# Hybrid decoder trunk, two layers: router by token blocks, the second adaLN's sums moved into mixing, a float32 gather and a 19th weight slot

## The chip, the cores and the metric

One core of one Trainium2 chip runs the whole program. Times are device microseconds (us) of one execution; the median of three executions is given beside the one that was profiled.

Engines: TensorE (PE, with its weight loads shown apart as PEld), VectorE (DVE), ScalarE (ACT), GpSimd (POOL) and SyncE (SP). SP's queue issues all transfers of weights; DMA engines move the bytes.

## What is computed

Two layers over 256 tokens of width 1024, all in float32:

```python
for l in range(DEPTH):
    mod = (silu(c) @ w_ada[l] + b_ada[l])[:, None, :]
    sh1, sc1, gt1, sh2, sc2, gt2 = jnp.split(mod, 6, axis=-1)
    h = x * (1 + sc1) + sh1
    q, k, v, u, vs = jnp.split(h @ w_in[l], split_at, axis=-1)
    att = rms_norm(diff_attention(rope(q), rope(k), v, lam), subln_g[l]) * (1.0 - lam_init)
    sg = chunk_spatial_gate(gelu(u), gelu(vs), sg_ln_g[l], sg_ln_b[l], w_spatial[l], b_spatial[l])
    mix = jnp.concatenate([att, sg], axis=-1) @ w_out[l]
    x = layer_norm(DEEPNORM_ALPHA * x + (1 + gt1) * mix, ln1_g[l], ln1_b[l])
    h = x * (1 + sc2) + sh2
    ffn = hier_moe(h, ...)      # top 1 of 4 groups, then top 2 of its 8 experts, SwiGLU with 512 inner columns
    x = layer_norm(DEEPNORM_ALPHA * x + (1 + gt2) * ffn, ln2_g[l], ln2_b[l])
```

The weights of all 32 experts of a layer are 6 MiB each, so nearly all of the 468 MB that are moved are expert weights.

## The kernel before

**Weights.** All weights form one list of transfers of up to 1 MiB (`stream`), in the order in which the program uses them. `pump` (the `dma_start` of line 180) puts them into a ring of `RING = 18` slots, in the order of the list: transfer n waits for the release of a slot, which `done` reports when the last reader of an older transfer has been issued. An expert without tokens is skipped on the chip by a condition on its transfers. The list of a layer is: w_in by sections (Q, K, VS, U, V), pieces of w_ada between them, w_out, more of w_ada, and then the experts' gate, up and down weights.

**Tokens.** The 256 tokens are two blocks of 128 (`tci` 0 and 1), a token a partition. `X` holds them as [128, 2, 8, 128]: column d = 8p + k of a token stands at [k, p], so that a fixed k gives 128 contiguous numbers, and the view `Xn` that goes over a token's 512 columns in natural order has a stride. `transpose_X` turns X into blocks with 128 columns on partitions, and `make_hT` applies adaLN's scale and shift in the copy out of PSUM, shared between DVE and ACT.

**Mixing.** `mixing` runs the sections (L594), attention and gating, and then the output projection `wo` (L861): 16 records per pair (`tci`, `hf`), first those that read gating (`hf` = 1) for both blocks, with `att_T` (L737, L738) between, then those that read attention. `residual` (L887, L889) multiplies by the gate and adds to X, `normalise` takes the statistics (L556) and normalises in place (L558).

**adaLN.** c times a w_ada column piece is a sum over 1024 rows. One part is folded ahead of time on DVE (`ada_fold`, L446: a scaled addition of one 512-column piece to an accumulator, done a few at a time by `fold_on`) or on POOL (`ada_fold_too`), the other is summed on PE (`ada_sum`: L411 for the accumulator, L416 for the rest). `ada_cols` turns the row into columns by transposes (L430), `affine_cols` makes scale and shift (`gc`, `bc`) of them. For the second adaLN (`s2`) four of eight pieces are folded in `mixing`, and `routing` does the rest.

**Routing and gather.** `routing` makes, between the normalised X and the router's logits: s2's sums and columns; a split of X into three bfloat16 parts (`Xp`; casts on ACT L920 to L937, subtractions on POOL L922 to L938), which together are X to float32's accuracy; the transposed hT; the logits with the router's 36 columns stationary and 256 tokens moving (L944), over two halves of the partitions, which are copied (L946, L947) and added by a matmul with the constant `fold` (L952); and the copy of the logits (L955). Then DVE finds the chosen experts and each token's position in its expert's slots. `selection` makes 0/1 matrices `G` (L1124), and `gather` multiplies the three parts of X by G (L1150) and applies gc and bc on the way out of PSUM (L1156 on DVE, L1159 on ACT).

**Experts.** `experts` runs 11 units: six of 2 experts with 64 slots each, then five of 4 experts with 32. A unit does gate and up (`proj`, L1171), silu and product (L1215, L1225), transposes (L1237, L1239), down (L1259), the multiplication by the gate (L1265) and the scatter back to the tokens (L1180). `gather` for the next two units follows the gate of every odd unit. `rescale` and `add_x` (L1187, alpha X through PE into the same sum) come in the last units. `spill` is the branch for experts with more tokens than slots; it isn't taken with these inputs.

Of the kernel before, what the change touches and what calls it, by code (L numbers as in the profile page):

```python
# [8 lines left out]
F32 = mybir.dt.float32  # L9
# [3 lines left out]
ALU = mybir.AluOpType  # L13
# [5 lines left out]
RING = 18  # L19
# [8 lines left out]
def kernel(  # L28
# [105 lines left out]
    for l in range(L):  # L134
# [26 lines left out]

    def pump(limit=RING):
# [48 lines left out]
    X = const.tile([P, NTC, KD, P], F32, name="X")  # L211
    fp = front_pool(0)
    xin = fp.tile([P, NTC, D], F32, tag="hT", name="xin")
    def Xn(tci, half=None):
        v = X[:, tci] if half is None else X[:, tci, :, half * 64:(half + 1) * 64]
        return v.rearrange("t k p -> t p k")
# [5 lines left out]
    for tci in range(NTC):  # L222
        nc.sync.dma_start(xin[:, tci, :], x[0, tci * P:(tci + 1) * P, :])
# [48 lines left out]
    fold = const.tile([P, NG + NE], F32, name="fold")  # L272
    V.tensor_tensor(fold, ident[:, 0:NG + NE], ident[:, 64:64 + NG + NE], op=ALU.add)
# [163 lines left out]
    def ada_fold(l, part):  # L437
        acc = held["ada", l, part, 0][:, 0, :]
        for k in range(4):
# [112 lines left out]
    def normalise(tci):  # L552
        st = small.tile([P, 2, 6], F32, tag="bnst", name="bnst")
        flat = X[:, tci].rearrange("t k p -> t (k p)")
        for h in range(2):
            V.bn_stats(st[:, h, :], flat[:, h * 512:(h + 1) * 512])  # L556
        mu, rs = mean_rstd(st)
        V.tensor_scalar(flat, flat, mu, rs, op0=ALU.subtract, op1=ALU.mult)  # L558


    def normalise_psum(tci, ps, st):
# [3 lines left out]
        S.activation(Xn(tci, 1), ps[1].rearrange("t (p k) -> t p k", k=KD), AF.Identity, scale=rs, bias=nm)  # L565
        V.tensor_scalar(Xn(tci, 0), ps[0].rearrange("t (p k) -> t p k", k=KD), mu, rs,  # L566
# [21 lines left out]
    def mixing(l, fp, y_prev, sts):  # L588
        hT = fp.tile([P, KD, NT], F32, tag="hT", name="hT")
# [797 lines left out]
```

## Time and profile before

| | |
|---|---|
| median of three executions | 1234.27 us (1232.76 to 1234.47) |
| the profiled execution | 1234.19 us |
| its span in the trace | 1232.57 us |
| PE busy | 1052.1 us (85%) |
| DVE busy | 347.1 us (28%) |
| ACT busy | 169.5 us (14%) |
| POOL busy | 73.2 us (6%) |
| DMA | 467.62 MB, mean 379 GB/s |

The span is what the trace covers; 1.6 us of the execution lie around it. The busy shares are means over stages that have different limits, so the views that count are those by stretch (busy time of each engine, granted PE clock, share of the DMA engines and GB/s) and the timeline, in which a row is a run of like instructions with its start, its length, its count and, in brackets, the idle time of the engine ahead of it and what released it.

Layer 0 lies about from 0 to 620 us, layer 1 from there to the end. In each the mixing comes first (to about 175 and 755 us), then routing (to about 198 and 778 us), then the experts.

### The profile page before, as it was taken

What the parts mean: (1) busy time and instruction counts of PE and PEld (TensorE: products, weight loads), DVE (VectorE), ACT (ScalarE), POOL (GpSimd) and SP (SyncE); (2) the same over time, 40 slices, a digit from 0 to 9 for tenths busy, and PEclk for the clock granted to TensorE, in tenths of its full rate; (3) what the DMA queues carried; (4) which work ended last, traced back from release to release, by engine and by line L of the source; (5) the groups of instructions that cost most, each with busy time, mean ns of one, the idle gap of its engine ahead of it and who ended that gap; (6) DMA issues with size and microseconds to landing.
All of it is one profiled execution on the core that took longest, in us unless ns stands there. A gap on an engine that the chain in (4) does not pass through costs nothing. (4 is left out here: it accounts for less than half of the span.)

```text
span 1232.6 us, 14266 instructions
## 1 busy us (share of the span) xinstructions
PE 1052.1 (85%) x5318; PEld 417.9 (34%) x5320; DVE 347.1 (28%) x803; ACT 169.5 (14%) x401; POOL 73.2 (6%) x52
## 2 busy tenths in 40 slices
PE   5999798899999686778789997989999868778875
PEld 1465343434343131122234653443434213112221
DVE  0386357412111010031045546631112101003103
ACT  1135513101010010000021322210101001000000
POOL 0204511000000000000000302000000000000000
PEclk8899898999999898999999999999999989898998
DMA  9998778899999999999999927889999999999995
GB/s 354 365 409 307 294 280 349 347 405 420 422 420 422 421 421 421 421 422 420 400 396 397 388 86 276 348 343 403 422 421 421 420 422 420 421 421 421 420 411 201
DMA packets 89262, 467.62 MB, mean 379 GB/s; under 512 B 12301, under 2 KB 12817, under 8 KB 40290
## 3 DMA queue, kind: packets, MB, share of 16 engines
q1 hardware_dynamic: 88818, 465.85, 93.6%
q8 instruction: 45, 0.74, 0.2%
q10 hardware_dynamic: 288, 0.52, 0.1%
q0 software_dynamic: 80, 0.26, 0.1%
q14 instruction: 31, 0.25, 0.1%
HBM read 484.43 MB, written 1.05 MB: 394 GB/s over the span
## 5 line engine op out<-in xcount | busy, mean ns | idle before, releaser
L1259 PE MATMUL dps<-w,eaT_moe 128*32 128x512 f32 (+1 forms) x1024 | 202.2, 648 | 45.7 <-DMA w<-in_w_down_dram 36.9
L1171 PE MATMUL up<-w,XT_moe 128*32 128x512 f32 (+1 forms) x1024 | 188.9, 620 | 33.0 <-DMA w<-in_w_up_dram 33.0
L1171 PE MATMUL gate<-w,XT_moe 128*32 128x512 f32 (+1 forms) x1024 | 187.5, 644 | 26.6 <-DMA w<-in_w_gate_dram 26.6
L594 PE MATMUL sec<-w,hT_front 128*128 128x512 f32 x256 | 115.8, 606 | 3.8 <-DVE X L566 2.2
L1259 PEld LDWEIGHTS dps<-w,eaT_moe 128*32 128x32 f32 (+1 forms) x1024 | 53.2, 127 | 177.1 <-issue 98.9
L1171 PEld LDWEIGHTS up<-w,XT_moe 128*32 128x32 f32 (+1 forms) x1024 | 51.4, 123 | 160.5 <-issue 99.3
L1171 PEld LDWEIGHTS gate<-w,XT_moe 128*32 128x32 f32 (+1 forms) x1024 | 52.7, 127 | 155.0 <-issue 105.7
L1225 DVE TENSOR_TENSOR act_moe<-sg_moe,up 128x512 f32<-128x512 f32 x22 | 15.1, 688 | 315.2 <-PE up L1171 280.5
L1265 DVE TENSOR_TENSOR eo_moe<-dps,gt 128x512 f32<-128x512 f32 x44 | 30.4, 692 | 213.6 <-PE dps L1259 213.6
L1180 PE MATMUL y<-eo_moe,wt_moe 128*128 128x512 f32 x176 | 84.9, 607 | 1.6 <-DVE eo_moe L1265 1.6
L1215 ACT ACTIVATE sg_moe<-gate 128x512 f32<-128x512 f32 x22 | 13.1, 597 | 412.6 <-PE gate L1171 412.5
L594 PEld LDWEIGHTS sec<-w,hT_front 128*128 128x128 f32 x256 | 48.6, 195 | 61.8 <-issue 53.9
L1150 PE MATMUL gps<-G_moe,Xp_moe 128*128 128x256 bf16 (+1 forms) x672 | 64.6, 250 | 3.7 <-DVE XT_moe L1156 1.8
L1156 DVE TENSOR_SCALAR XT_moe<-gps,gc,bc 128x128 f32<-128x128 f32 x88 | 30.6, 404 | 120.8 <-PE gps L1150 120.8
L1150 PEld LDWEIGHTS <-Xp_moe 128*128 128x128 bf16 x672 | 53.1, 97 | 22.0 <-issue 13.1
L1195 ACT COPY wt_moe<-wtps 128x256 f32<-128x256 f32 x22 | 8.2, 372 | 275.1 <-PE wtps L1193 275.1
L1180 PEld LDWEIGHTS y<-eo_moe,wt_moe 128*128 128x128 f32 x176 | 30.3, 191 | 43.6 <-issue 40.2
L1159 ACT ACTIVATE XT_moe<-gps,bc,gc 128x128 f32<-128x128 f32 x88 | 33.7, 455 | 41.9 <-PE gps L1150 41.9
L462 POOL TENSOR_TENSOR w<-w,w 128x2048 f32<-128x2048 f32 x7 | 31.6, 4521 | 56.2 <-ACT w L458 45.6
L416 PE MATMUL ada_s<-w,csl 128*32 128x512 f32 x128 | 20.8, 765 | 12.8 <-DMA w<-in_w_ada_dram 12.8
L861 PE MATMUL wo<-w,zu_front 128*128 128x512 f32 x64 | 30.6, 635 | 0.0
L755 PE MATMUL u<-hT_front,w 128*128 128x256 f32 x128 | 28.8, 379 | 0.0
(275 smaller groups left out, 762.2 us busy)
## 6 DMA issues: line engine op xcount, KB each, us to landing
w<-in_w_gate_dram SPq DMA_DIRECT2D x128, 1024.0 KB
w<-in_w_up_dram SPq DMA_DIRECT2D x128, 1024.0 KB
w<-in_w_down_dram SPq DMA_DIRECT2D x120, 1024.0 KB
w<-in_w_ada_dram SPq DMA_DIRECT2D x48, 1024.0 KB
w<-in_w_in_dram SPq DMA_DIRECT2D x20, 1024.0 KB
w<-in_w_out_dram SPq DMA_DIRECT2D x8, 1024.0 KB
w<-in_w_down_dram SPq DMA_DIRECT2D x16, 512.0 KB
xin_front<-in_x_dram SPq DMA_DIRECT2D x2, 512.0 KB
```

Source lines behind the costliest of these rows:

```text
L416: T.matmul(ps[32 * j:32 * j + 32], cs(k), held["ada", l, part, k][:, 0, j * 512:(j + 1) * 512], start=(k == 0), stop=(k == KD - 1))
L462: G.tensor_tensor(acc, acc, w, op=ALU.add)
L594: T.matmul(ps, hT[:, k, tci * P:(tci + 1) * P], held["in", l, s, k // 4][:, k % 4, :], start=(k == 0), stop=(k == KD - 1))
L755: T.matmul(ps[:, 0:NT], held["in", l, U_, k // 4][:, k % 4, g * P:(g + 1) * P], hT[:, k, :], start=(k == 0), stop=(k == KD - 1))
L861: T.matmul(o_ps[tci][h], (cat, zu)[hf][:, kk, tci * P:(tci + 1) * P], w[:, kk, :], start=(hf == 1 and kk == 0), stop=(hf == 0 and kk == 3))
L1150: T.matmul(ps[:, k - kk].rearrange("p j s -> p (j s)"), parts[:, a, tci, k, :], g[:, tci, js[0] * P:(js[-1] + 1) * P], start=(a == 0 and t ...
L1156: V.tensor_scalar(dst, ps[:, k - kk, i, :], gc[:, k:k + 1], bc[:, k:k + 1], op0=ALU.mult, op1=ALU.add)
L1159: S.activation(dst, ps[:, k - kk, i, :], AF.Identity, scale=gc[:, k:k + 1], bias=bc[:, k:k + 1])
L1171: T.matmul(ps[c0:c0 + w], xt[:, k, c0:c0 + w], held[nm, l, place, k // 4][:, k % 4, :], start=(k == 0), stop=(k == KD - 1))
L1180: T.matmul(y[tci][h], wt[:, tci, :], eo[:, h, :], start=(i == 0), stop=(i == NU - 1))
L1259: T.matmul(dps[h][s0:s0 + w], aT[:, kk, s0:s0 + w], held["down", l, place, part][:, kk - ks[0], c0:c0 + 512], start=(kk == 0), stop=(kk == ...
L1265: V.tensor_tensor(eo[:, h, :], dps[h], gt2[:, h * 512:(h + 1) * 512], op=ALU.mult)
```

## The change

- `RING` is 19. The last slot (`LENT`) holds the sections' input hT in mixing; the stream may use it only for keys of a layer whose V section has been issued (`lent["layer"]`).
- `X` is [128, 2, 1024] in natural order. `Xn` is contiguous, and `Xk` (one k) takes every eighth number. x is loaded into X directly, without the copies.
- In the list, s2's pieces 4 to 7 stand ahead of w_out. In layer 1 all eight pieces of s2 are folded on DVE; `fold_on` is called with 8, 8, 8, 4 and 5.
- `ada_sum` of s2 stands behind wo's `hf` = 1 records of block 0, `ada_cols` and `affine_cols` behind those of block 1.
- Statistics of a half of a block are taken right behind its residual. At layer 1's entry the statistics of the last quarter of y come behind the first block's normalisation.
- The router's logits are made by token block: 128 columns of hT stationary, the router's 36 columns moving, into the sum that starts with the bias. The two halves on partitions, their copies and `fold` are gone. hT of block 0 is written by ACT alone.
- The gather multiplies float32 X by float32 G: two matmuls for each k where there were six in bfloat16. The three parts and their casts and subtractions are gone.
- The last gather moves to unit NU-3, its selection to NU-4. `spill` is written anew, with its output added through PE (not taken here), and stands ahead of `rescale`.

```diff
-RING = 18
+RING = 19
+LENT = RING - 1
@@
+        add_ada(l, "s2", range(4, 8))
         add_out(l)
-        add_ada(l, "s2", range(4, 8))
         add_ada(l, "g2", range(4))
@@ pump
-            slot_of[key] = free.pop(0)
+            fit = [i for i in free if i != LENT or key[1] <= lent["layer"]]
+            if not fit:
+                break
+            slot_of[key] = fit[0]
+            free.remove(fit[0])
@@
-    X = const.tile([P, NTC, KD, P], F32, name="X")
+    X = const.tile([P, NTC, D], F32, name="X")
+    def Xn(tci, half):
+        return X[:, tci, half * 512:(half + 1) * 512]
+    def Xk(tci, k):
+        return X[:, tci, k::KD]
@@ ada_fold
-        for k in range(4):
+        for k in range(4 if l == 0 else KD):
@@ transpose_X
-            T.transpose(ps[:, k, :], X[:, tci, kk + k, :], ident)
+            T.transpose(ps[:, k, :], Xk(tci, kk + k), ident)
@@ mixing
-        hT = fp.tile([P, KD, NT], F32, tag="hT", name="hT")
+        hT = slots[LENT].rearrange("p (k t) -> p k t", k=KD)
...
             normalise_psum(0, y_prev[0], sts[0])
+            V.bn_stats(sts[1][:, 1, :], y_prev[1][1])
...
         rescale_part(2)
-        fold_on(17)
+        fold_on(8)
...
         scores(3)
-        S.copy(vv[:, 1, :], section(l, V_, 1))
+        v1 = section(l, V_, 1)
+        lent["layer"] = l
+        pump()
+        S.copy(vv[:, 1, :], v1)
         fold_too(8)
+        fold_on(4)
...
+        fold_on(5)
         a_T(2)
         a_T(3)
...
             for h in range(2):
                 wo(tci, h, 1)
+            if tci == 0:
+                asum2 = ada_sum(l, "s2", KD // 2 if l == 0 else KD)
+            else:
+                ada_cols(l, 2, asum2, fp)
+                affine2 = affine_cols(l, 1)
             att_T(tci, ats[tci])
...
                 residual(tci, h, o_ps[tci][h], gt1, fp)
-            normalise(tci)
+                V.bn_stats(st[:, h, :], Xn(tci, h))
+            normalise(tci, st)
@@ routing
-        ada_cols(l, 2, ada_sum(l, "s2", KD // 2), fp)
-        gc, bc = affine_cols(l, 1)
-        S.copy(parts[:, 0, 0], X[:, 0])
...
-        G.tensor_tensor(rem[0], X[:, 0], parts[:, 0, 0], op=ALU.subtract)
...
+        def logits(tci):
+            spread(lgp[:, tci], R_RT, l * NL, NL, True, False)
+            for k in range(KD):
+                T.matmul(lgp[:, tci], hk(k)[:, tci * P:(tci + 1) * P], wr[:, k, :], start=False, stop=(k == KD - 1))
...
+        make_hT(hk, gc, bc, 0, early, both=False)
+        gsum = gate_sum(l, "g2", 5)
+        logits(0)
+        for kk in (0, 4):
+            early[1, kk] = transpose_X(pm, "m", 1, kk)
+        make_hT(hk, gc, bc, 1, early)
+        logits(1)
...
         V.tensor_copy(lg, lgp)
-        gsum = gate_sum(l, "g2", 5, gate_sum(l, "g2", 5))
+        gate_sum(l, "g2", 5, gsum)
@@ selection
-            g = mp.tile([P, NTC, 2 * P], BF16, tag="G", name=f"G{q}")
+            g = mp.tile([P, NTC, 2 * P], F32, tag="G", name=f"G{q}")
@@ gather
-                    for a in range(3):
-                        for tci in range(NTC):
-                            T.matmul(ps[:, k - kk].rearrange("p j s -> p (j s)"), parts[:, a, tci, k, :],
-                                     g[:, tci, js[0] * P:(js[-1] + 1) * P], start=(a == 0 and tci == 0), stop=(a == 2 and tci == NTC - 1))
+                    for tci in range(NTC):
+                        T.matmul(ps[:, k - kk].rearrange("p j s -> p (j s)"), Xk(tci, k),
+                                 g[:, tci, js[0] * P:(js[-1] + 1) * P], start=(tci == 0), stop=(tci == NTC - 1))
@@ experts
-            if i % 2 == 1 and i // 2 + 1 < NQ:
-                gather(i // 2 + 1, range(len(UNITS[i + 1:i + 3])))
+            if (i % 2 == 1 and i // 2 + 1 < NQ - 1) or i == NU - 3:
+                q = (i + 1) // 2 if i < NU - 3 else NQ - 1
+                gather(q, range(len(UNITS[2 * q:2 * q + 2])))
...
+            if i == NU - 4:
+                selection(NQ - 1)
```

## Rows read from the trace of the kernel before

**Rows 1.** Windows: us, busy us of PE, PEld, DVE, ACT, POOL, PE clock, DMA share, GB/s.

```profile
95.00:240.00 145.00, 123.42 (x620) 60.02 (x622) 81.85 (x189) 47.14 (x121) 40.42 (x12) 0.92 0.80 308
...
226.00:232.00 6.00, 6.00 (x22) 2.02 (x24) 2.58 (x3) 0.00 (x0) 0.00 (x0) 0.74 0.18 72
...
695.00:822.00 127.00, 114.21 (x586) 57.34 (x586) 69.04 (x183) 31.33 (x94) 13.97 (x9) 0.96 0.67 261
...
822.00:1205.00 383.00, 327.61 (x1740) 111.09 (x1738) 53.34 (x100) 25.19 (x58) 0.00 (x0) 0.95 1.01 418
```

**Rows 2.** Timeline, layer 0, w_ada's requests and PE: start us, us, engine, line, operation.

```profile
105.86 32.98 SPq L180 DMA_DIRECT2D w<-in_w_ada_dram  x8
...
136.62 7.03 PE L861 MATMUL wo<-w,zu_front 128*128 128x512 f32 x16
...
148.07 1.09 PE L737 MATMUL attT<-ident,at_front 128*128 128x128 f32 x4 [4.42 <-DVE rsv L526]
...
148.95 9.53 PE L861 MATMUL wo<-w,zu_front 128*128 128x512 f32 x16
...
163.38 1.04 PE L430 MATMUL adaT<-ident,adar_front 128*64 128x128 f32 x8
...
176.41 3.62 PE L416 MATMUL ada_s<-w,csl 128*32 128x512 f32 x32
```

**Rows 3.** Timeline, layer 0, from wo's last records to the logits.

```profile
164.25 10.47 PE L861 MATMUL wo<-w,cg_front 128*128 128x512 f32 x24
...
175.05 0.68 DVE L887 TENSOR_TENSOR res_front<-wo,cg_front 128x512 f32<-128x512 f32 x1
...
175.76 1.10 DVE L889 TENSOR_TENSOR X<-X,res_front 128x512 f32<-128x512 f32 x1
...
176.89 1.29 DVE L556 BATCH_NORM_STATS2 bnst<-X 128x6 f32<-128x512 f32 x2
...
179.75 0.81 DVE L558 TENSOR_SCALAR X<-X,mv,rs 128x1024 f32<-128x1024 f32 x1
...
186.44 1.50 ACT L585 ACTIVATE hT_moe<-hTps,bc,gc 128x128 f32<-128x128 f32 x4 [3.88 <-DVE gc L520]
...
193.61 0.23 DVE L955 COPY lgbig_moe<-rt 128x72 f32<-128x72 f32 x1 [1.16 <-PE rt L952]
```

**Rows 4.** Timeline, layer 1: entry, attention's copies, normalised X, logits.

```profile
629.83 1.21 ACT L565 ACTIVATE X<-y,nm,rs 128x512 f32<-128x512 f32 x1 [0.86 <-DVE nm L564]
...
721.98 1.02 DVE L713 COPY aT_front<-aTps 128x384 f32<-128x384 f32 x2 [0.44 <-PE aTps L711]
...
759.23 0.81 DVE L558 TENSOR_SCALAR X<-X,mv,rs 128x1024 f32<-128x1024 f32 x1
...
773.35 0.23 DVE L955 COPY lgbig_moe<-rt 128x72 f32<-128x72 f32 x1 [1.16 <-PE rt L952]
```

**Rows 5.** Timeline, layer 0, PE: first gather, unit 0's down, first gather of two units.

```profile
198.32 1.50 PE L1150 MATMUL gps<-G_moe,Xp_moe 128*128 128x128 bf16 x24 [0.77 <-DVE G_moe L1124]
...
225.86 8.66 PE L1259 MATMUL dps<-w,eaT_moe 128*64 128x512 f32 x32 [3.78 <-issue]
...
241.32 2.79 PE L1150 MATMUL gps<-G_moe,Xp_moe 128*128 128x256 bf16 x24
```

**Rows 6.** Timeline, layer 0, PE: float32 records of 128 columns.

```profile
96.33 1.05 PE L747 MATMUL mix<-wsp_front,zv_front 128*128 128x128 f32 x8 [0.16 <-issue]
```

**Rows 7.** Groups by line and form: busy us, mean ns, then idle us ahead of them.

```profile
L1180 PE MATMUL y<-eo_moe,wt_moe 128*128 128x512 f32 x176 | 84.9, 607 | 1.6 <-DVE eo_moe L1265 1.6
...
L1187 PE MATMUL y<-X,ident 128*128 128x512 f32 x16 | 14.4, 1056 | 5.4 <-PEq L1070 4.3 <-DVEq L1070 1.1
...
L1237 PEld LDWEIGHTS atps<-ident,act_moe 128*128 128x128 f32 x88 | 13.6, 204 | 12.1 <-issue 8.0 <-DVE act_moe L1225 3.5 <-DVE G_moe L1124 0.5
...
L430 PEld LDWEIGHTS adaT<-ident,adar_moe 128*64 128x64 f32 x16 | 1.7, 135 | 3.2 <-issue 1.6 <-ACT adar_moe L425 1.6
...
L446 DVE SCALAR_TENSOR_TENSOR w<-w,csl,w 128x512 f32<-128x512 f32 x24 | 16.2, 744 | 0.0
```

More of the change, by code (lines that the diff above doesn't have):

```diff
@@ L160 @@
     later = []
+    lent = {"layer": -1}
     def pump(limit=RING):
@@ L550, in mean_rstd, with normalise @@
         return mv[:, 0:1], rs
[L552 to L556, printed above, removed]
+    def normalise(tci, st):
         mu, rs = mean_rstd(st)
-        V.tensor_scalar(flat, flat, mu, rs, op0=ALU.subtract, op1=ALU.mult)
+        V.tensor_scalar(X[:, tci], X[:, tci], mu, rs, op0=ALU.subtract, op1=ALU.mult)
     def normalise_psum(tci, ps, st):
@@ L572, in transpose_X, with make_hT @@
         for k in range(4):
-            T.transpose(ps[:, k, :], X[:, tci, kk + k, :], ident)
+            T.transpose(ps[:, k, :], Xk(tci, kk + k), ident)
         return ps
-    def make_hT(dst_k, gc, bc, tci, early=None):
+    def make_hT(dst_k, gc, bc, tci, early=None, both=True):
         for kk in range(0, KD, 4):
@@ L581, in make_hT @@
                 dst = dst_k(k)[:, tci * P:(tci + 1) * P]
-                if kk == 0:
+                if kk == 0 and both:
                     V.tensor_scalar(dst, ps[:, i, :], gc[:, k:k + 1], bc[:, k:k + 1], op0=ALU.mult, op1=ALU.add)
@@ L770, in rescale_part @@
             for tci in range(NTC):
-                G.tensor_tensor(Xn(tci, h), Xn(tci, h), row.rearrange("t (p k) -> t p k", k=KD), op=op)
+                G.tensor_tensor(Xn(tci, h), Xn(tci, h), row, op=op)
         folds = ada_fold(l, "s2")
@@ L1070, in spill @@
         with tc.If(n > SLOTS):
-            parts = Xp.bitcast(BF16).rearrange("t k (a c d) -> t a c k d", a=3, c=NTC)
-            for k in range(KD):
-                for tci in range(NTC):
-                    for a in range(3):
-                        T.matmul(ps[:, tci * P:(tci + 1) * P], parts[:, a, tci, k, :], identb,
-                                 start=(a == 0), stop=(a == 2))
-                S.activation(Xp[:, k, 0:NT], ps[:, 0:NT], AF.Identity, scale=gc[:, k:k + 1], bias=bc[:, k:k + 1])
@@ L1097, in spill @@
                             V.tensor_scalar_mul(t, ps, ovc[:, tci, bass.ds(e, 1)])
                             V.tensor_tensor(t, t, gt[:, h * 512:(h + 1) * 512], op=ALU.mult)
-                            xv = Xn(tci, h)
-                            V.tensor_tensor(xv, xv, t.rearrange("t (p k) -> t p k", k=KD), op=ALU.add)
+                            T.matmul(y[tci][h], ident, t, start=False, stop=False)
     def last_rows(l, mp):
         fg = mp.tile([P, D], F32, tag="XT", name="fing", bufs=3)
-        fb = mp.tile([P, D], F32, tag="Xp", name="finb")
+        fb = mp.tile([P, D], F32, tag="XT", name="finb", bufs=3)
@@ L1228, in experts @@
                 gather(0, (1,))
-            if i % 2 == 0 and i // 2 + 1 < NQ:
+            if i % 2 == 0 and i // 2 + 1 < NQ - 1:
                 if i == 0:
@@ L1283, in experts @@
             scatter(NU - 1, tci, (1,))
-            V.bn_stats(st[:, tci, 1, :], y[tci][1])
+            if tci == 0 or l + 1 == L:
+                V.bn_stats(st[:, tci, 1, :], y[tci][1])
         sts = [st[:, tci] for tci in range(NTC)]
@@ L1297 @@
                 f()
-            def x_in():
-                for tci in range(NTC):
-                    (V.tensor_copy if tci else S.copy)(X[:, tci], xin[:, tci].rearrange("t (p k) -> t k p", k=KD))
             def first_X(k):
-                if k == 3:
-                    x_in()
-                elif k == 5:
+                if k == 5:
                     for tci in range(NTC):
@@ L1315 @@
             load_spatial(l, fp)
[L1316 removed]
+        affine2 = mixing(l, fp, y, sts)
         fp.stack.close()
         mp = moe_pool(l)
[L1319 to L1320 removed]
+        gc, bc, posm, rest, places, gsum = routing(l, wrs[l], affine2, mp)
+        y, sts, fin = experts(l, gc, bc, posm, rest, places, gsum, mp)
         if l + 1 == L:
@@ L1327 @@
             rs = small.tile([P, NTC], F32, tag="frs", name="frs")
-            os = [mp.tile([P, D], F32, tag="XT", name=f"o{tci}", bufs=3) for tci in range(NTC)]
+            os = [mp.tile([P, D], F32, tag=tag, name=f"o_{tag}", bufs=n) for tag, n in (("XT", 3), ("eo", 1))]
             pieces = [(tci, h, slice(h * 512, (h + 1) * 512)) for tci in range(NTC) for h in range(2)]
```

113 lines of the change are left out of this document (39 added, 74 removed).

## The prediction

> **What bounds the kernel now.** I read the windows by stage first [rows 1]. From 240 us on in layer 0, and in the stretch shown of layer 1, the DMA engines work without a pause (share 1.01, 418 GB/s, so a 1 MiB transfer takes 1.0486 MB / 418 GB/s = 2.51 us) while PE is busy 86% of the time: these stretches can't shorten unless fewer bytes are read, and the change reads the same bytes. The two fronts are different: 95 to 240 us moves 308 GB/s at a share of 0.80, 695 to 822 us 261 GB/s at 0.67, with PE the busiest engine. There the ring is full and a transfer waits until PE has used up an older slot. The last large gap of layer 0 is 226 to 232 us (0.18), while unit 0's down holds the slots. So a layer gains what its PE is earlier at the first downs, and a further slot is worth one more transfer in flight at the last gap: 2.51 us. The tail behind the last transfer isn't on the list: add_x and the last gather lie ahead of it, under the saturated DMA. The sum is thus a walk along PE's path in the two fronts, and I read that path in the timeline.
>
> **Layer 0.** *Second adaLN's sums.* Before, ada_s (3.62 us, and about 1.0 for the eight bias records ahead of it) stands in routing [rows 2]. Moved behind the 16 first records of wo, it falls into the 4.42 us in which PE waits for attT's input (the row at 148.07). 4.6 us into 4.4 us: nothing. It also keeps PE busy: the 16 records behind that idle took 9.53 us, the 16 ahead of it 7.03, with a granted clock of 0.92 in the stretch as a whole [rows 1]; if the clock stays up, −2.5. The eight adaT transposes, before in routing, now stand among the wo records: eight take 1.04 (the row at 163.38), +0.9. w_out is now requested where those four pieces of s2 were, as the first four of eight requests spread over 32.98 us from 105.86 on [rows 2], so by about 122, and is in by about 130, ahead of wo at 136.62: nothing; had it to wait for the eighth, at 139, some 5. Sum at the end of wo: −1.6. Bounds: +1.0 (clock as before) to −1.7.
>
> *Block 1 from wo's end to X normalised.* PE ends wo at 174.72, X is normalised at 180.56: 5.84 us [rows 3]. The add on strided X takes 1.10 us, an operation of the same size on contiguous data 0.68: −0.4. The two bn_stats (1.29) stood behind both halves; one now runs while PE works on the other half: −0.65. The DVE queue ahead of it gets shorter by as much again in block 0, of which I take 0.4. Sum −1.5 (−1.0 to −1.9).
>
> *X normalised to logits copied.* Before: 180.56 to 193.61 = 13.05 us, in which ACT waits 3.88 us for gc, behind it the transposed blocks, 16 records, two copies and the fold [rows 3]. After, gc is long there. What is left: eight transposes 1.1, hand-over to ACT 0.7, four ACT writes 1.5 (the row at 186.44; DVE does the other four beside it), bias and that half of the 16 records of 128 stationary columns which can't start before, 1.3 at some 0.12 us each (eight such take 1.05, of which the last is 0.27 [rows 6]: 0.11 from one to the next), hand-over to DVE 0.9: 5.5 us. −7.5 (−6 to −8.5). The four ACT casts and four POOL subtracts vanish; neither is waited for once the gather reads X.
>
> Layer 0 at the logits: −1.6 − 1.5 − 7.5 = **−10.6**.
>
> **Layer 1.** *Entry.* bn_stats of the second block leaves the path to the first normalised X (0.65), the ACT write (1.21 into strided X, some 0.6 contiguous) and the DVE write of the second (0.44 less) get shorter; as the row of the first ACT write shows, transposes and all behind them follow it at once [rows 4]. −1.7 (−0.5 to −2).
>
> *The eight more folds.* In layer 1 all eight pieces of s2 are folded on DVE: 16 more operations at 16.2 / 24 = 0.68 us each [rows 7]. Eight come behind u_part(2), where I find DVE idle (it is busy 69 of the front's 127 us [rows 1]); without that idle they would cost 5.4. The other eight stand in DVE's queue ahead of the aT copies, which before started 0.44 us behind PE's transposes at 721.98 [rows 4]: 8 × 0.68 = 5.4 less that 0.44 = +5.0, and att(2) and wo on PE wait for those copies. In exchange PE's sum is 8 records and not 40. There is no idle in this layer ahead of attT, so bias records and adaT count in full: +1.7. Bounds of the fold: 0 (if the scores keep PE behind it) to +5.4.
>
> *wo to X normalised* as in layer 0: −1.1 (no clock to gain, and the DVE queue was shorter). *X to logits*: 760.04 to 773.35 = 13.3 before [rows 4], 5.5 after: −7.8.
>
> Layer 1 at the logits: −1.7 + 5.0 + 1.7 − 1.1 − 7.8 = **−3.9**.
>
> **Both layers, gathers.** Before, a unit's gather of 64 slots is 48 bf16 records (two rows of 24; 1.50 us the first) [rows 5], after it 32 float32 records (8 k, 2 blocks, 2 passes) of 128 columns. At 0.11 us each that is 3.6 against 3.0: +0.6 for the first unit, and +0.3 for the second, since most of it hides under the 3.78 us that PE waits for eaT. The pair's gather of 256 columns, two such rows as the one at 241.32 (5.6 us together), becomes 32 records at half of what one of 512 columns takes (7.03 / 16 = 0.44 [rows 2]): 32 × 0.22 = 7.0, +1.4, ahead of unit 1's down, so it counts. Together +2.3. The 19th slot: −2.5. Behind that, PE has 14% to spare under the saturated DMA [rows 1], so later gathers, add_x, the moved last gather and its selection cost nothing; uncovered, the five later pair gathers would be +1.4 each.
>
> *The unknown price* is the stationary load from X[:, tci, k::8], one float32 in every 32 bytes, which no row has at 128 columns. Lower bound: contiguous, the load hidden at 0.11 a step [rows 6]; a gain is excluded, since a step holds as many elements. The nearest rows above: 128 columns at 16 bytes apart take 204 ns, and 64 columns at 32 bytes 135 ns [rows 7]; with the latter's kind, eight transposes still went in 1.04 us [rows 2]. Strided *moving* data cost far more: 1056 ns for 512 columns of X at 512 bytes apart [rows 7], against 607 for 512 contiguous ones in the scatter, so 0.88 ns a column more; on 128 columns that is +0.11. Upper bound: nothing of the load hidden, 0.204 + 0.11 = 0.31. I take 0.11, by the 64-column row, which is the same stride.
>
> The Trainium skill (Advanced Engine Details and Errata, section SBUF Cachelines) says that an access pattern which touches a different 16-byte line with each element is slowed, and that two hits a line are needed for full speed. The trace agrees where X is moved (1056 ns) and leaves it open for stationary loads. By that rule the new gather runs as the first rival below has it.
>
> **Sum.** Layer 0: −10.6 + 2.3 − 2.5 = −10.8. Layer 1: −3.9 + 2.3 − 2.5 = −4.1. Together −14.9, since layer 1's front starts from the end of layer 0's transfers. The profiled execution took 1234.19 us (span 1232.57), the median is 1234.27: 1234.2 − 14.9 = **1219**; with the bounds of the terms, 1215 to 1223.
>
> **Rivals.**
> 1. *Strided loads at half rate*, 0.22 us a record as moving X shows. First gather +3.4, second +2.0 (past its cover), transposes in routing +0.8: 6.2 a layer, so 1219 + 12.4 = 1231. For it: the moving row. Against it: the 64-column loads, which show nothing of it.
> 2. *Slower: the load of X lies wholly in the open*, 0.31 us a record. 32 × 0.2 = 6.4 for the first gather, 6.4 − 2 for the second, 32 × 0.09 = 2.9 for the 256-column one, 8 × 0.2 = 1.6 for transposes: 15.3 a layer, 1219 + 31 = 1250. The mean gain of 7.5 a layer is used up at about 0.235 us a record (0.125 × 32 × 2 − 2 + 0.015 × 32 + 1.0 = 7.5); beyond that the change is a loss. Against it: loads overlap matmuls throughout (in 95 to 240 us PE is busy 123 us and its loads 60, more than the stretch holds in series [rows 1]).
> 3. *The folds cost nothing* (PE itself is later at the copies): 1214.
> 4. *The 19th slot does nothing*, for instance because a layer 1 key may not take it and blocks those behind, or the gap is one of bandwidth: 1219 + 5 = 1224.
>
> **Chances.** Forecast 0.60, rival 1 0.17, rival 2 0.09, rival 3 0.05, rival 4 0.09. The predicted time is the forecast's, 1219. The range 1213.5 to 1233 takes in rivals 1, 3 and 4, and leaves out rival 2 and a tenth of the rest. A measurement of this kernel can tell 0.2% (2.5 us) from no change, so "same" is 1231.8 to 1236.7: the forecast, rivals 3 and 4 and some half of rival 1 lie below (0.80), the rest of rival 1 and the lower end of rival 2 within (0.09), the remainder above (0.11).
>
> **What would show it.** Logits copied 5.5 us behind the normalised X in both layers (13 before); no idle of PE ahead of attT in layer 0 and its next 16 wo records in about 7 us; in layer 1 eight folds on DVE ahead of the aT copies, with PE idle some 5 us behind the transposes; the first gather at 32 float32 records with 0.11 us from one to the next, against 0.216 or 0.31; the DMA share in 95 to 240 us above 0.80 and the gap behind 226 us shorter. I am wrong if the step of the gather is above 0.2, if the ada sum doesn't fit into attT's wait, or if the DMA is saturated no earlier than before in spite of an earlier gather.

## The result and the profile after

The changed kernel takes 1247.26 us (median of 4 executions, 1246.75 to 1248.34) against 1234.37 for the kernel before: a ratio of 1.0101 with the interval 1.0074 to 1.0128, slower by some 13 us. The forecast was 1219, the range 1213.5 to 1233. The profiled execution has a span of 1245.9 us against 1232.57.

First the windows of the changed kernel (columns as in [rows 1]):

```profile
95.00:240.00 145.00, 133.66 (x605) 70.89 (x605) 75.59 (x184) 44.25 (x121) 31.68 (x7) 0.94 0.81 322
...
695.00:822.00 127.00, 116.90 (x476) 66.78 (x477) 72.02 (x188) 28.00 (x92) 6.14 (x4) 0.89 0.62 235
822.00:1205.00 383.00, 335.32 (x1679) 130.02 (x1676) 50.77 (x100) 24.13 (x57) 0.00 (x0) 0.95 1.00 413
```

```profile
223.00:229.00 6.00, 6.00 (x16) 1.93 (x18) 2.60 (x3) 0.00 (x0) 0.00 (x0) 0.53 0.01 3
```

The DMA-bound stretch is what it was. In both fronts PE is busy for longer (133.7 for 123.4 us, 116.9 for 114.2), with fewer records, and the large gap at unit 0's down is still there and emptier (share 0.01, 0.18 before [rows 1]), at a granted clock of 0.53, near the lower of the two levels (1.2 of 2.4 GHz; 0.74 before). The front of layer 1 moves fewer bytes than before, at a granted clock of 0.89 for 0.96.

Then the path of layer 0, in the timeline (start us, us, engine, line, operation), the rows that answer to [rows 2], [rows 3] and [rows 5]:

```profile
144.29 3.62 PE L425 MATMUL ada_s<-w,csl 128*32 128x512 f32 x32
...
147.93 0.63 PE L743 MATMUL attT<-ident,at_front 128*128 128x128 f32 x4
...
148.40 7.03 PE L872 MATMUL wo<-w,zu_front 128*128 128x512 f32 x16
...
180.24 2.26 PE L942 MATMUL rt<-wr,hT_moe 128*128 128x36 f32 x16
...
182.53 0.23 DVE L955 COPY lgbig_moe<-rt 128x72 f32<-128x72 f32 x1 [1.40 <-PE rt L942]
...
187.24 7.92 PE L1142 MATMUL gps<-G_moe,X 128*128 128x128 f32 x32 [0.77 <-DVE G_moe L1117]
...
222.89 9.95 PE L1254 MATMUL dps<-w,eaT_moe 128*64 128x512 f32 x32 [2.79 <-issue]
```

```profile
239.63 8.07 PE L1142 MATMUL gps<-G_moe,X 128*128 128x256 f32 x32
```

Up to the logits all is as forecast: the sums fill the wait ahead of attT, the next 16 records of wo take 7.03 us where they took 9.53 [rows 2], and the logits are copied at 182.53 for 193.61 [rows 3]. Then the gather: 32 records in 7.92 us, 0.245 from one to the next, where two rows of 24 like that in [rows 5] took 3.1. With 256 moving columns it is about the same, 0.25 (8.07 us for 32): not what is moved but what is loaded sets the pace.

The path of layer 1, the rows that answer to [rows 4]:

```profile
635.46 8.50 PE L599 MATMUL sec<-w,w 128*128 128x512 f32 x16 [2.39 <-DMA w<-in_w_in_dram]
...
722.49 5.38 DVE L455 SCALAR_TENSOR_TENSOR w<-w,csl,w 128x512 f32<-128x512 f32 x8
```

```profile
728.40 3.78 PE L502 MATMUL gtps<-gr_front,selg 128*128 128x512 f32 x4 [4.98 <-DVE aT_front L719]
```

and the first section as it was in the kernel before:

```profile
636.41 7.11 PE L594 MATMUL sec<-w,hT_front 128*128 128x512 f32 x16 [2.17 <-DVE X L566]
```

The folds stand ahead of the aT copies and PE waits 4.98 us (0.33 before), as forecast (+5.0). What was not: PE is slower behind the wait (gtps 3.78 us), and the sections now wait for the weights of w_in, so the earlier normalised X is worth nothing. Nor are the eight folds behind u_part(2) hidden. Beside POOL's additions to X, contiguous here, they take 8.89 us and not 5.38, and four records of the scores behind them take 1.08 us:

```profile
691.75 8.89 DVE L455 SCALAR_TENSOR_TENSOR w<-w,csl,w 128x512 f32<-128x512 f32 x8
...
701.29 1.08 PE L684 MATMUL s<-qk_front 64*128 64x128 f32 x4
```

In the run with four folds below, which has no folds there, the same four records take 0.49 us and the scores end 0.7 us sooner behind their start. The clock in three stretches behind waits of PE (the sections, gtps and att, the logits; windows of layer 1, columns as in [rows 1]):

```profile
635.50:640.00 4.50, 4.50 (x8) 1.99 (x9) 0.00 (x0) 0.00 (x0) 0.00 (x0) 0.69 1.05 387
...
728.40:733.00 4.60, 4.60 (x9) 2.53 (x10) 0.41 (x1) 1.37 (x2) 0.00 (x0) 0.50 1.01 427
771.00:776.00 5.00, 5.00 (x27) 4.94 (x26) 1.37 (x4) 1.50 (x4) 0.00 (x0) 0.54 0.74 298
```

PE is busy throughout all three and is granted 0.69, 0.50 and 0.54. The waits ahead of them are 2.39, 4.98 and, for the logits, only 0.49 us.

The walk of the prediction against the two traces, in us earlier (−) or later (+) than before at each point; layer 1 is counted from layer 0's last down:

| point on PE's path | layer 0 forecast | layer 0 measured | layer 1 forecast | layer 1 measured |
|---|---|---|---|---|
| sections begin | 0 | +0.2 | −1.7 | +0.3 |
| sections end | 0 | −0.2 | −1.7 | +2.4 |
| att(3) done | 0 | −0.2 | +3.3 | +9.7 |
| wo done | −1.6 | −1.9 | +5.0 | +12.1 |
| logits copied | −10.6 | −11.1 | −3.9 | +4.5 |
| unit 0's gate begins | −10.0 | −6.4 | −3.3 | +9.2 |
| unit 0's down begins | −9.7 | −3.0 | −3.0 | +12.6 |
| unit 1's down begins | −8.3 | +0.5 | −1.6 | +15.9 |
| last down | −10.8 | −1.3 | −4.1 | +14.5 |

### The profile page after: what moved, and what is told of

Its sections match the earlier page's. It is cut to its first block, busy times and chain, and to the rows that moved or that the text cites. A ratio compares the mean times of both kernels' runs of the same rounds, so it can differ in the third digit from the quotient of the medians.

```text
span 1245.9 us, 13799 instructions
## 1 busy us (share of the span) xinstructions
PE 1088.2 (87%) x5086; PEld 476.3 (38%) x5088; DVE 339.9 (27%) x807; ACT 160.9 (13%) x398; POOL 54.8 (4%) x42
## 3 DMA queue, kind: packets, MB, share of 16 engines
HBM read 484.43 MB, written 1.05 MB: 390 GB/s over the span
## 5 line engine op out<-in xcount | busy, mean ns | idle before, releaser
L1163 PE MATMUL gate<-w,XT_moe 128*32 128x512 f32 (+1 forms) x1024 | 194.1, 648 | 34.0 <-DMA w<-in_w_gate_dram 33.9
L1163 PE MATMUL up<-w,XT_moe 128*32 128x512 f32 (+1 forms) x1024 | 174.2, 604 | 18.7 <-DMA w<-in_w_up_dram 18.7
L599 PE MATMUL sec<-w,w 128*128 128x512 f32 x256 | 116.7, 611 | 3.9 <-DMA w<-in_w_in_dram 2.4
L1142 PE MATMUL gps<-G_moe,X 128*128 128x256 f32 (+1 forms) x448 | 111.9, 411 | 1.5 <-DVE G_moe L1117 1.5
L1142 PEld LDWEIGHTS gps<-G_moe,X 128*128 128x128 f32 x448 | 108.4, 335 | 11.5 <-issue 8.2
L599 PEld LDWEIGHTS sec<-w,w 128*128 128x128 f32 x256 | 49.1, 197 | 62.5 <-issue 57.6
L455 DVE SCALAR_TENSOR_TENSOR w<-w,csl,w 128x512 f32<-128x512 f32 x40 | 30.4, 831 | 0.0
L425 PE MATMUL ada_s<-w,csl 128*32 128x512 f32 x96 | 16.8, 807 | 14.4 <-DMA w<-in_w_ada_dram 14.4
L761 PE MATMUL u<-w,w 128*128 128x256 f32 x128 | 28.8, 379 | 0.0
```

The lines of the kernel that those rows point to most:

```text
L425: T.matmul(ps[32 * j:32 * j + 32], cs(k), held["ada", l, part, k][:, 0, j * 512:(j + 1) * 512], start=(k == 0), stop=(k == KD - 1))
L455: yield V.scalar_tensor_tensor(acc[:, c], w[:, c], csl[:, k:k + 1], acc[:, c], op0=ALU.mult, op1=ALU.add)
L599: T.matmul(ps, hT[:, k, tci * P:(tci + 1) * P], held["in", l, s, k // 4][:, k % 4, :], start=(k == 0), stop=(k == KD - 1))
L761: T.matmul(ps[:, 0:NT], held["in", l, U_, k // 4][:, k % 4, g * P:(g + 1) * P], hT[:, k, :], start=(k == 0), stop=(k == KD - 1))
L1142: T.matmul(ps[:, k - kk].rearrange("p j s -> p (j s)"), Xk(tci, k), g[:, tci, js[0] * P:(js[-1] + 1) * P], start=(tci == 0), stop=(tci == ...
L1163: T.matmul(ps[c0:c0 + w], xt[:, k, c0:c0 + w], held[nm, l, place, k // 4][:, k % 4, :], start=(k == 0), stop=(k == KD - 1))
```

## The experiments

Theory 1: the price of the gather is that of loading stationary float32 columns that lie 32 bytes apart. Theory 2: the folds ahead of the aT copies cost layer 1 their own length and a slower clock behind it. Rivals: float32 on both sides is slow in itself; the wait only uncovers another; the slot does nothing. Each run is a few lines away from the changed kernel.

### X by k: contiguous stationary columns

```diff
-    X = const.tile([P, NTC, D], F32, name="X")
+    X = const.tile([P, NTC, KD, P], F32, name="X")
...
-        return X[:, tci, half * 512:(half + 1) * 512]
+        return X[:, tci, :, half * 64:(half + 1) * 64].rearrange("t k p -> t p k")
...
-        return X[:, tci, k::KD]
+        return X[:, tci, k]
```

(x is loaded into the lent slot and copied; additions to X go through a strided view and the statistics are taken behind both halves, as before the change.)

> The changed kernel with X kept by k as before (128 contiguous numbers for each k), all else as changed. Theory 1, the stationary load of strided X sets the pace of the gather: its float32 records fall from 0.245 us to 0.11 at 128 columns and to 0.22 at 256, which is 4.3 + 3.4 + 0.8 us earlier at the first downs of each layer; against it the strided residual adds and the statistics behind both halves give back some 1.5 a layer. Net about 7 a layer: 1233 us (1229 to 1238). Rival, float32 operands on both sides are slow in themselves: records stay at 0.245 and the time is 1247 to 1250.

Measured: 1240.50 us, later than the expected 1229 to 1238; ratio to the kernel before 1.0064 (1.0037 to 1.0091). Its timeline, layer 0 (PE) and layer 1 (DVE, POOL, PE):

```profile
180.19 3.33 PE L949 MATMUL rt<-wr,hT_moe 128*128 128x36 f32 x16 [1.71 <-ACT hT_moe L595]
...
185.15 3.61 PE L949 MATMUL rt<-wr,hT_moe 128*128 128x36 f32 x16
...
193.49 4.11 PE L1149 MATMUL gps<-G_moe,X 128*128 128x128 f32 x32 [0.77 <-DVE G_moe L1124]
```

```profile
688.62 11.56 DVE L459 SCALAR_TENSOR_TENSOR w<-w,csl,w 128x512 f32<-128x512 f32 x8
...
691.51 7.48 POOL L782 TENSOR_TENSOR X<-X,rsrow_front 128x512 f32<-128x512 f32 x4 [1.55 <-ACT rsrow_front L780]
...
700.84 1.39 PE L689 MATMUL s<-qk_front 64*128 64x128 f32 x4 [2.72 <-DVE zu_front L761]
```

The same 32 float32 records take 4.11 us: theory 1 holds, its rival falls. But only 6.8 of the 14 us come back. Two places took the rest. The first is routing: from wo's end to the logits this run takes 13.3 us in layer 0 and 13.4 in layer 1, the changed kernel 9.7 and 11.5. PE waits 1.71 us ahead of the logits of block 0 (0.43 in the changed kernel), and the 16 logit records of block 1 take 3.61 us, where the changed kernel's layer 0 is done with them in 2.26; from 183.30 to 188.60 us the granted clock is 0.50. The clock there isn't the layout's alone, though. The run with four folds below does in layer 0 just what the changed kernel does, with the same wait of 0.43 us, and has

```profile
183.21 3.61 PE L942 MATMUL rt<-wr,hT_moe 128*128 128x36 f32 x16
```

so X to logits takes 7.26 us there and 5.15 in the changed kernel, with the same code.

The second place is layer 1, where the folds behind u_part(2), which I had put down as hidden, take 11.56 us for eight while POOL adds to X with a stride (8.89 beside the contiguous additions of the changed kernel, 5.38 alone). POOL's four strided additions take 5.96 us where no folds stand beside them, so 11.56 is about the sum of the two: side by side they gain next to nothing. PE waits 2.72 us for DVE there.

### The stationary load by itself

```diff
+            for j in range(16): T.matmul(pp[:, 0:128], pt[:, j % 2:j % 2 + 128:1], ident, start=True, stop=True)
+            for j in range(16): T.matmul(pp[:, 0:128], pt[:, j % 2:j % 2 + 256:2], ident, start=True, stop=True)
...
+            for j in range(32): T.matmul(pp[:, 0:128], pb[:, j % 2:j % 2 + 2048:16], identb, start=True, stop=True)
             ada_cols(0, 0, ada_sum(0, "s1", 0, first_X), fp)
```

> The changed kernel with rows of matmuls on a constant tile put ahead of the first adaLN's sums (their results go nowhere; the time is longer by what they take). They measure the step from record to record by the distance of the stationary columns: float32 128 x 128 at 4, 8, 16 and 32 bytes; 64 columns at 32 bytes; 128 columns at 32 bytes with 256 and 512 moving columns; transposes at 4, 16 and 32 bytes; bfloat16 at 2, 4, 8, 16 and 32 bytes. Theory 1a, a float32 matmul record loads its stationary block in two halves of 0.12 us each when columns lie apart, a transpose only one: 0.24 a record at 32 bytes for 128 columns whatever moves up to 256, 0.43 with 512 moving (hidden), 0.12 for 64 columns and for transposes, 0.11 contiguous. Theory 1b, the price is the gather's place in the program (other traffic into the same memory): all records here take 0.11 to 0.13 at 128 moving columns.

The execution takes 1304.43 us with the added rows. Its timeline on PE; in order: float32, 128 stationary columns at 4, 8, 16, 32 bytes; 64 columns at 32; 128 at 32 bytes with 256 and with 512 moving; transposes at 4, 16, 32 bytes; bfloat16 at 2 bytes and, after three rows left out, at 32; the last row only ends the one ahead of it:

```profile
27.90 3.73 PE L1306 MATMUL probe<-ident,w 128*128 128x128 f32 x32
31.48 3.93 PE L1307 MATMUL probe<-ident,w 128*128 128x128 f32 x32
35.24 7.63 PE L1308 MATMUL probe<-ident,w 128*128 128x128 f32 x32
42.71 7.84 PE L1309 MATMUL probe<-ident,w 128*128 128x128 f32 x32
50.48 4.11 PE L1310 MATMUL probe<-ident,w 128*64 128x128 f32 x32
54.52 7.98 PE L1311 MATMUL probe<-w 128*128 128x256 f32 x32
62.34 7.05 PE L1312 MATMUL probe<-w 128*128 128x512 f32 x16
69.23 1.91 PE L1313 MATMUL probe<-ident,w 128*128 128x128 f32 x16
70.97 2.08 PE L1314 MATMUL probe<-ident,w 128*128 128x128 f32 x16
72.89 1.96 PE L1315 MATMUL probe<-ident,w 128*128 128x128 f32 x16
74.69 1.95 PE L1316 MATMUL probe<-identb,w 128*128 128x128 bf16 x32
...
82.01 2.16 PE L1320 MATMUL probe<-identb,w 128*128 128x128 bf16 x32
84.10 5.36 PE L425 MATMUL ada_s<-w,csl 128*32 128x512 f32 x48
```

From start to start, divided by the records: float32 0.112 us at 4 bytes, 0.118 at 8, 0.233 at 16 and 0.243 at 32. 64 columns at 32 bytes 0.126. With 256 moving columns 0.244, with 512 0.43: there the load is hidden. A transpose takes 0.109, 0.120 and 0.113. bfloat16 takes 0.056 at 2 bytes and 0.065 at 32. The granted clock is 1.00 in all these rows. So the price is that of a float32 matmul record with 128 stationary columns 16 or 32 bytes apart, some 1.9 ns a column; half the columns, a transpose, or more work per load hide most of it. Theory 1b (the place in the program) falls: the records are as slow here as in the gather.

### The folds behind the aT copies

```diff
         fold_too(8)
-        fold_on(4)
...
-        fold_on(5)
         a_T(2)
         a_T(3)
+        fold_on(9)
```

> The changed kernel with the last nine folds of the second adaLN issued behind the aT copies of scores 2 and 3 instead of ahead of them. Theory 2, the eight folds of layer 1 ahead of the copies cost PE 5 us of waiting and the slower clock behind that another 3: the 4.98 us idle ahead of gtps vanishes, gtps takes 2.0 and not 3.8 us, and the time falls by 8 to 1239 us (1237 to 1242). Rival, the wait only moves (ada_s then waits for the folds, or the clock falls elsewhere): 1243 to 1248.

Measured: 1239.84 us, ratio 1.0034 (1.0019 to 1.0049): 7.4 us earlier than the changed kernel, as theory 2 has it. Its timeline (PE, DVE):

```profile
727.34 1.98 PE L502 MATMUL gtps<-gr_front,selg 128*128 128x512 f32 x4 [0.32 <-DVE aT_front L719]
```

```profile
727.67 5.38 DVE L455 SCALAR_TENSOR_TENSOR w<-w,csl,w 128x512 f32<-128x512 f32 x8
```

The same 5.38 us of folds now lie under gtps, att and wo, nobody waits for them, and gtps is back at 1.98.

### Both

The two diffs above together.

> Both of the edits above. If the two causes are separate and both are on PE's path, their gains add up: 1247 - 14 - 8 = 1225 us (1221 to 1231), faster than the kernel before. If they hide each other, 1233 or later.

Measured: 1233.72 us, ratio 0.9986 (0.9971 to 1.0001). The two gains add up to what each gave alone (6.8 + 7.4 = 14.2, measured 13.5): the causes are separate. The time alone would fit the expectation's other branch (1233 or later), but that it is 1234 and not 1225 is in the main the shortfall of X by k, 6.8 for 14.

### Four folds in layer 1 as in layer 0

```diff
-        for k in range(4 if l == 0 else KD):
+        for k in range(4):
...
-                asum2 = ada_sum(l, "s2", KD // 2 if l == 0 else KD)
+                asum2 = ada_sum(l, "s2", KD // 2)
```

> The changed kernel, but with only four pieces of the second adaLN folded on DVE in layer 1 too (as in layer 0), the other four summed on PE. Theory 2 (eight folds ahead of the aT copies stall PE by 5 us and cost 3 more in clock): both go, 32 records or 3.6 us come back on PE: 1247 - 8 + 3.6 = 1243 us (1240 to 1245). Rival (the folds only uncover a wait that is there anyway): 1247 to 1251.

Measured: 1242.90 us, ratio 1.0055 (1.0034 to 1.0076); the wait ahead of gtps is gone and ada_s has 40 records in the path, 4.4 us less in all. The same edit with X by k:

> X kept by k (contiguous stationary columns) and only four pieces folded in layer 1. In the run with X by k and the folds behind the copies, layer 1 lost 2.7 us of PE to DVE ahead of the scores and a slower clock behind it, where eight folds on DVE and the strided additions to X on POOL run side by side. If those folds are the cause, that goes too: 1240.5 - 8 + 3.6 - 4 = 1232 us (1229 to 1235). If the strided additions alone are the cause: 1236 (1235 to 1238).

Measured: 1229.55 us, ratio 0.9957 (0.9929 to 0.9986), 11 us below X by k alone and not 4.4. Of the further 6.6 us the rows show 5.3 as the collision of DVE's folds with POOL's strided additions: from the first scores to the end of the section behind them X by k takes 15.8 us, this run 9.8, the changed kernel 10.5 and its run with four folds 9.8. Without those folds the POOL rows and the scores read

```profile
691.70 3.01 POOL L782 TENSOR_TENSOR X<-X,rsrow_front 128x512 f32<-128x512 f32 x2 [0.76 <-ACT rsrow_front L780]
...
693.00 0.49 PE L689 MATMUL s<-qk_front 64*128 64x128 f32 x4
```

with no wait of PE.

### The 19th slot not lent

```diff
-        lent["layer"] = l
         pump()
```

> The changed kernel in which the 19th slot is never lent to the stream: it holds the sections' input and nothing else, so the ring has 18 slots throughout. By the prediction's step a slot is worth one transfer in flight at a layer's last gap, 2.5 us: 1247 + 5 = 1252 us (1250 to 1254). Rival 4 of the prediction (the slot does nothing): 1246 to 1248.

Measured: 1254.01 us, ratio 1.0138 (1.0095 to 1.018), 6.8 us more than the changed kernel. From unit 1's down to the layer's last down the changed kernel gains 1.8 and 1.4 us on the kernel before, this one loses 0.8 and 0.3: the slot is worth 2.6 and 1.8 us in the two layers. The rest, some 2 us, lies ahead of that point in layer 0 (unit 1's down begins at 261.11 for 258.97) and isn't shown to be the slot's: 1.4 of it is there already among the first sections (51.40 for 50.02 us), long before the slot is lent, and the run with four folds, whose layer 0 is the changed kernel's, begins unit 1's down at 262.83. The prediction's 2.5 a layer was of the right size; rival 4 falls.

### Two forms of X and 18 slots

The second form takes the room of one slot; the folds stand behind the copies.

```diff
-RING = 19
+RING = 18
...
-        V.tensor_scalar(X[:, tci], X[:, tci], mu, rs, op0=ALU.subtract, op1=ALU.mult)
+        V.tensor_scalar(X[:, tci], xf[0][:, tci].rearrange("t (p k) -> t k p", k=KD), mu, rs, op0=ALU.subtract, op1=ALU.mult)
```

> Two forms of X: natural order in the mixing stage (contiguous additions, statistics by halves), and by k from the normalisation on (contiguous stationary columns for transposes and gather). The second form takes the place of one slot, so the ring has 18 with the sections' input in the last (17 in the front). The last nine folds stand behind the aT copies. Against X by k with the folds behind (1233.7 us): routing 2 us a layer earlier, the 2.7 us wait ahead of the scores and its clock 4 to 5, one slot less +2.5 a layer: 1230 us (1226 to 1234). If 17 slots starve the front, 1236 or later.

Measured: 1239.37 us, ratio 1.0027 (1.0008 to 1.0046), a miss by 9 us: it is 5.7 us later than X by k with the folds behind. The traces of the two runs show what came and what didn't. The contiguous additions gave 3.7 us in layer 1, of the 4 to 5 expected (91.9 us for 95.6 from the sections' begin to att(3)). Routing's 2 us a layer did not come: wo's end to the logits takes 14.0 and 14.1 us, in the other run 13.5 in both layers. And from unit 1's down to the last down, where the run above shows the slot's worth, this run loses 5.2 and 1.7 us. That 17 slots starve the front, as the expectation's other branch had it (1236 or later), is not what happened: from the third section of layer 0 (50.51 and 46.73 us) to wo's end both take 122.9 us.

### The folds in DVE's waits

X by k, eight folds on, the last sixteen in other places:

```diff
+            fold_on(2)
             V.reciprocal(sm, sm)
...
         rescale_part(2)
-        fold_on(8)
...
-        fold_on(4)
...
-        fold_on(5)
         a_T(2)
         a_T(3)
+        fold_on(9)
```

> X by k, all eight pieces folded in layer 1, but the last sixteen folds put where DVE waits: two in each of the four scores between the negated maximum and the reciprocal, where DVE stands 1.87 us for ACT's exponentials, and the rest behind the aT copies. If folds cost nothing in DVE's waits, layer 1 keeps what four folds gave (no stall, no collision with POOL's additions) and has 3.6 us less on PE (8 records of ada_s and not 40): 1229.5 - 3.6 = 1226 us (1223 to 1229). If the waits are too short for them or DVE and POOL collide again, 1230 to 1234.

Measured: 1228.17 us, ratio 0.9953 (0.9934 to 0.9971), within the expected range but only 1.4 us below four folds, which the two intervals don't tell apart. Its timeline on DVE:

```profile
701.36 1.41 DVE L459 SCALAR_TENSOR_TENSOR w<-w,csl,w 128x512 f32<-128x512 f32 x2
...
703.32 0.18 DVE L708 RECIPROCAL smx<-smx 128x4 f32<-128x4 f32 x1 [0.55 <-ACT e_front L705]
```

Two folds fit into the wait for ACT's exponentials and leave 0.55 us of it. From layer 0's last down to X normalised in layer 1 this trace takes 3.4 us less than the one with four folds, near the 3.6 expected; the medians don't show it.

### Statistics by halves

```diff
                 residual(tci, h, o_ps[tci][h], gt1, fp)
-            flat = X[:, tci].rearrange("t k p -> t (k p)")
-            for h in range(2):
-                V.bn_stats(st[:, h, :], flat[:, h * 512:(h + 1) * 512])
+                V.bn_stats(st[:, h, :], X[:, tci, :, h * 64:(h + 1) * 64])
             normalise(tci, st)
```

> As the run with X by k and the folds in DVE's waits, and the statistics of a half of a block taken right behind its residual, over eight pieces of 64 numbers. In the runs with X by k, PE waited 1.71 us in routing ahead of the logits of block 0 and ran at half clock behind it (16 records in 3.3 to 3.6 us for 2.3 to 2.9). If the statistics behind both halves are what makes it wait: 0.7 us of statistics and 2 to 3 us of clock come back in each layer, 1228 - 6 = 1222 us (1219 to 1225). If the strided additions to X suffice for the wait, the clock stays low: 1226 to 1228.

Measured: 1223.78 us, in the expected range; ratio 0.9906 (0.9878 to 0.9935): faster than both kernels, by 10.6 us than the one before. It is 4.4 us below the run above, whose interval (0.9934 to 0.9971) just touches this one. The logit records of the two blocks in layer 0, in this run and then in the one above:

```profile
177.35 2.85 PE L946 MATMUL rt<-wr,hT_moe 128*128 128x36 f32 x16 [1.24 <-ACT hT_moe L595]
...
181.25 2.26 PE L946 MATMUL rt<-wr,hT_moe 128*128 128x36 f32 x16
```

```profile
177.56 2.86 PE L948 MATMUL rt<-wr,hT_moe 128*128 128x36 f32 x16 [1.70 <-ACT hT_moe L595]
...
181.84 3.61 PE L948 MATMUL rt<-wr,hT_moe 128*128 128x36 f32 x16
```

the windows of the same stretch, this run first:

```profile
180.00:183.50 3.50, 3.38 (x31) 3.08 (x34) 1.37 (x4) 1.50 (x4) 0.00 (x0) 1.00 1.02 424
```

```profile
180.00:185.40 5.40, 5.40 (x32) 5.27 (x31) 1.36 (x4) 1.51 (x4) 0.00 (x0) 0.55 1.01 422
```

and block 1's logits in layer 1, this run first:

```profile
761.60 3.61 PE L946 MATMUL rt<-wr,hT_moe 128*128 128x36 f32 x16
```

```profile
764.44 3.63 PE L948 MATMUL rt<-wr,hT_moe 128*128 128x36 f32 x16
```

The statistics themselves are worth 0.47 us in both layers: X of block 1 is normalised 5.35 us behind wo's end for 5.82, and PE's wait ahead of block 0's logits is 0.46 us shorter. The clock is another matter. In layer 0 it is 1.00 for 0.55 and the logits come 5.11 us behind X for 6.85; in layer 1 of the same trace the records are as slow as in the run above, and the logits come 7.51 us behind X for 6.41. So it isn't shown that the statistics give the clock back, and with what the changed kernel's own code does there (5.15 and 7.26 us in the two traces above) it can't be read from one layer of one trace. Where the 4.4 us of the medians come from stays open beyond the 0.47 a layer.

## Why the prediction was wrong, point by point

**The step that failed is the unknown price.** I took 0.11 us a record for the stationary load at 32 bytes, by the nearest row with the same stride, the adaT transposes. That row was wrong on two counts at once: it loads half the columns, and a transpose isn't a float32 matmul. The probe gives 0.126 for the first, 0.113 for the second, and 0.243 where neither holds. The other row I had, 204 ns for act's columns at 16 bytes [rows 7], was of transposes too, and I held it against the wrong row: the transposes of X, contiguous in the kernel before, load the same 128 columns in 141 ns, so 204 already showed the stride (the probe has 141 for transposes at 4 bytes and 208 at 16):

```profile
L573 PEld LDWEIGHTS hTps<-ident,X 128*128 128x128 f32 x64 | 7.2, 141 | 7.2 <-issue 4.3 <-ACT X L565 2.5 <-DVE res_front L887 0.5
```

In the changed kernel a load takes 335 ns in the gather, but 196 in the transposes of the same strided X (groups by line and form):

```profile
L1142 PEld LDWEIGHTS gps<-G_moe,X 128*128 128x128 f32 x448 | 108.4, 335 | 11.5 <-issue 8.2 <-DVE G_moe L1117 1.8 <-ACT gt L503 1.5
...
L578 PEld LDWEIGHTS hTps<-ident,X 128*128 128x128 f32 x64 | 8.6, 196 | 4.6 <-issue 2.9 <-ACT X L570 1.3 <-DMA X<-in_x_dram 0.3
```

The moving row (1056 ns), which I put into rival 1 at 0.22, was the better witness. The bounds held (0.11 to 0.31), the choice between them didn't. The break-even that rival 2 named, 0.235, is just passed by 0.245; without the 8.4 us of layer 1's front (below) the change would be some 5 us slower, not 13. That 1247 lies close to rival 2's 1250 is chance: its price of 0.31 was not measured, and the front of layer 1, which it didn't have, fills the difference.

**The gathers.** Forecast +2.3 a layer, measured in layer 0 +4.7 (first), +3.4 (second), +2.2 (pair). Rival 1 had the rate nearly (0.22 for 0.245) and 6.2 us a layer on top of the forecast; the trace has 8.0. The cover failed: PE's wait ahead of unit 0's down shrank by only 1.0 of its 3.78 us. The down waits for DVE's copy of eaT, and that stands in DVE's queue behind the gather's copies: from the last of those to eaT DVE takes 5.2 us in both kernels (219.86 to 225.07 before, 216.89 to 222.10 after), so a later gather makes a later eaT. Then there is a term that the sum didn't have: the 32 records of that down took 9.95 us for 8.66, in the window with a granted clock of 0.53. In the four kernels with strided X the same records take 8.5 to 10.0 us in the two layers, in the five with X by k 8.5 to 8.8, in the one with two forms 9.4 and 8.8; why the clock falls there was not tried. So layer 0 gains 1.3 and not 10.8, though everything up to the logits was right to 0.5 us, in part by luck: of X to logits the forecast was 5.5 us, this trace has 5.15, and the run with four folds, with the same code in layer 0, 7.26.

**Layer 1's front**, 8.4 us off at the logits. The folds' wait was right (+5.0, measured 4.98 for 0.33). Wrong were: the entry (−1.7, measured +0.3), since the DMA is saturated there (share 1.05) and w_in's first piece comes when it comes; I looked at which engine PE waited for and not at what would be next. The folds behind u_part(2), at nothing in the sum: 0.7 in the scores. And the clock: 1.4 us in the first 16 records behind the wait for w_in (8.50 for 7.11), some 2.6 in gtps and att behind the folds, 1.4 in routing; a further 0.6 lies in wo's stretch. Of these, the clock behind the folds is shown by the run that moves them, the one in routing goes up and down with the same code. I had counted a clock gained where a wait vanishes (−2.5, which was right) and none lost where the change makes one.

**What held:** the sums of the second adaLN in attT's wait (−1.9 at wo's end for −1.6), the shorter way to the normalised X (−1.3 for −1.5 in layer 0, −1.2 for −1.1 in layer 1), X to logits in layer 0 (−7.9 for −7.5; in layer 1 −6.4 for −7.8), w_out four transfers later at no cost, the 19th slot (2.6 and 1.8 for 2.5). Rival 3 fell (PE waits for the folds), rival 4 fell.

**The sum corrected.** Layer 0: 4.1 + 3.1 + 0.8 us of gathers beyond the forecast, 1.3 of clock, 0.7 at the slot, less 0.5 ahead of them: 9.5. Layer 1: 8.4 + 9.1 of gathers and their clock + 1.1 at the slot: 18.6. Together 28.1, against 1247.3 − 1219 = 28.3.

**What stays open:** why the loss of X by k against the forecast is made up only to 1224 and not to 1219 by the last run. Its strided residual adds (1.05 us for 0.69) are on the path, and layer 1's entry is bound by the DMA; that the two make up the 5 us was not tried. Open too is what sets the clock in routing, which ran at either level with the same code.

## What to carry to other kernels

Before a layout makes a stationary operand strided, time that very kind of record, since a row with the same stride but half the columns or of a transpose hides the load. A step that ends a wait can give clock back and one that makes a wait can take it, so a stall is priced with the records behind it; and a stretch whose clock goes up and down with the same code is not read from one trace. Work put on an idle engine (the folds on DVE) goes behind what the next engine waits for, into its waits, and not beside GpSimd's pass over X, least of all a strided one.

## What the runs showed of the hardware

- A float32 matmul record with 128 stationary columns takes 0.112 us at 4 bytes, 0.118 at 8, 0.233 at 16, 0.243 at 32; a transpose 0.109 to 0.120 at 4, 16 and 32, a bfloat16 record 0.056 at 2 bytes and 0.065 at 32. The Trainium skill (Advanced Engine Details and Errata, section SBUF Cachelines) has lines of 16 bytes and wants two hits on each; the step between 8 and 16 bytes agrees. Transposes and bfloat16 records show little of it.
- A fold on DVE takes 0.67 us alone (5.38 for eight), 1.11 (8.89 for eight) while POOL adds to contiguous X and 1.44 (11.56 for eight) while it adds with a stride. POOL's own two contiguous additions take 2.49 us alone and 3.12 and 3.38 then; its four strided ones 5.96 alone and 7.48 then. The Trainium skill (GPSIMD Engine Reference, section Specifications) says that the two engines share their interfaces to the memory and that DVE's instructions with two inputs there contend with POOL; a fold has two, and the trace agrees.
- What a wait of PE costs can be more than its length: behind the 4.98 us wait the granted clock was 0.50 and gtps took 3.78 us, without the wait 1.98. It isn't always so: behind a wait of 0.43 us the logits of layer 0, with the same code, ran at 1.00 in the changed kernel and at 0.64 in the run with four folds.
